# Hybrid Fourier / HGRN2 / mixture-of-experts layer: projections as single F32 products, and expert weights moved in transfers of one, two or four units

## The chip, the cores and the metric

The kernel runs on one core of one Trainium2 chip. The metric is the device time of one execution, in microseconds (us). TensorE is called PE below, its weight loads PEld, VectorE DVE, ScalarE ACT, GpSimd POOL, and the queue of SyncE, which issues nearly every load, SP.

## The reference

One layer over 512 latent rows and 256 context rows of width 1024, one sample, all in float32:

```
h_ctx = modulate(rms_norm(ctx, g_mix), sh1c, sc1c)
h_lat = modulate(rms_norm(x, g_mix), sh1, sc1)
u, q, v, gf, gb, g = split_proj(h @ w_in, lb)            # 1024 x 3072, for both streams
rec = rec_mixer(...)                                     # 4 heads, gated linear recurrence, two directions
mix = concatenate([fourier_mix(u, w_fourier), rec]) @ w_out
x = x + gt1 * mix
x = x + gt2 * ec_moe(modulate(rms_norm(x, g_ffn), sh2, sc2), w_router, w_g, w_u, w_d)
return rms_norm(x, g_final)

def ec_moe(h, w_r, w_g, w_u, w_d):                       # 16 experts, 64 tokens each
    affinity = softmax(h @ w_r)
    gate, idx = top_k(swapaxes(affinity, 1, 2), cap)
    xs = h[idx]
    hid = silu(xs @ w_g) * (xs @ w_u)                    # 1024 x 2816, twice
    ye = (hid @ w_d) * gate                              # 2816 x 1024
    return segment_sum(ye, idx)
```

The weights of the experts are 16 x 3 x 1024 x 2816 floats, 553.6 MB, and each is read once.

## The kernel before

The work falls into two parts. The **front** runs from the first load to the routing (0 to 372 us): the modulation of the rows by a product of the condition with `w_ada`, the input projection, the recurrence heads, the Fourier groups, the output projection, the router. The **experts** follow (372 us to the end).

*Projections.* The input projection goes by segments of 512 columns: q, vc (context rows of v), ff and fb (both streams), v, g, u, in this order, each in four steps of 256 channels. A step is cut into units: one 128x128 block of weights (or of rows) against 512 columns. Counted in such units there are q 32, vc 16, ff 32, fb 32, v 32, g 32, u 32 and, for the output projection, 64: 272 in all; ff and fb also have 32 products of 256 columns each with the context rows. Each operand is held as a high part, rounded to the type that PE takes in a single pass (F32R), and a low part, the rest; `mm3` (L144 to L147) makes each unit of three products, high by high, low by high and high by low. The parts of the weights are made by `split` and `split_tile`: a copy on ACT for the high part and a subtraction on POOL or DVE for the low one (L304 to L309). Raw weight tiles have four buffers, and so have the high and the low ones; a segment asks for the next step's tile when it begins a step.

*Order.* Three stretches are in an order that is written out by hand (`manual_schedule`): the opening (modulation, q, vc), the heads, and the PE stream of output projection, routing and first gate product. Between them the Tile framework orders the instructions. In the heads the units of v, g, u, the Fourier groups and part of the output projection are fillers: between two steps of the heads `fill_to(TURN)` takes units until PE has 3.0 us of work by the units' stated costs (0.65 us for a unit of a projection).

*Experts.* For each expert, eight units of gate weights, eight of up weights and eight of down weights come in; a unit is 128 partitions x 2816 floats (1.44 MB). They go through a ring of 13 equal slots, 7 in memory that the front's left side gives back and 6 on the right. SP issues a load when the slot's last reader is done. The order on PE within an expert is gate (L1403), up (L1403), transposes of the hidden rows (hT, L1435), down (dn, L1455), combination (cb, L1464); for every second expert the rows of two experts are gathered (gp, L1375). In memory a unit of gate or up is one contiguous block, 128 rows of 11264 bytes; a unit of down takes 11264 bytes out of each 45056. The last expert's down weights come by blocks of columns, in runs of 1024 and 512 bytes (`down_last`, L1488).

The context states (`ctx_states`) use two rotating buffers with the tag `gcc`, which the second part of the modulation uses before: POOL's memset of such a buffer waits for the transfer `gt2b` that still reads it.

Of the kernel before, what the change touches and what calls it, by code (L numbers as in the profile page):

```python
# [30 lines left out]
NSLOT_L = 7  # L31
NSLOT_R = 6
# [17 lines left out]
VC_AT = ((2, 6), (2, 7))  # L50

# columns of the packed small operands
# [8 lines left out]
# and of its matrices  # L61
# [4 lines left out]
# columns of the packed shape constants  # L66
# [16 lines left out]
def hybrid_kernel(ctx: ExitStack, tc, x, ctxt, small, const, pos, w_ada, b_ada, w_in, w_out,  # L83
                  wg, wu, wd, out):
# [12 lines left out]
    # ------------------------------------------------------------------ memory that stays  # L97
# [39 lines left out]
    def split_tile(w, name, low=None):  # L137
        wh = wst.tile([P, 2, 512], F32R, tag="wh", bufs=SB, name=f"{name}h")
        wl = wst.tile([P, 2, 512], F32R, tag="wl", bufs=SB, name=f"{name}l")
        ns.copy(wh, w)  # L140
        (low or nv).tensor_tensor(wl, w, wh.bitcast(F32), op=ALU.subtract)
        return wh, wl
# [6 lines left out]
    def pick(pair, sl):  # L149
        return (pair[0][sl], pair[1][sl])  # L150
# [25 lines left out]
    class AdaFirst:  # L176
        """Shift and scale of the mixer for channel blocks 2n and 2n+1."""

        def __init__(self, n):
            self.n = n  # L180
            if n % 2 == 0:
                # the memory of the values and of the context's gates
                w = p1b.tile([P, 2, 4, 256], F32, tag="v", name=f"adaw{n}_v")
                self.w = [w[:, 0], w[:, 1]] + [pc.tile([P, 4, 256], F32, tag=f"fctx{d}", name=f"adaw{n}_{d}")
                                               for d in range(2)]
            else:
                self.w = [wst.tile([P, 4, 256], F32, tag="wh" if t % 2 else "wl", bufs=SB, name=f"adaw{n}_{t}")
                          for t in range(4)]
            for t in range(4):
                # half of the rows of both halves of the sum  # L190
# [18 lines left out]
        def finish(self):  # L209
# [8 lines left out]
            # row r of the pair, shift or scale, channel block  # L218
# [10 lines left out]
    # ------------------------------------------------------------------ normalise and transpose  # L229
    # the transposed rows wait in the memory of the gates  # L230
# [28 lines left out]
    # high and low parts, channel blocks 4-7 and 0-3  # L259
    hlA = hl.tile([P, 2, 4, S], F32R, name="hlA")  # L260
    hl2 = tc.alloc_tile_pool(name="hl2", bufs=1, side="right")
    hlB = hl2.tile([P, 2, 4, S], F32R, name="hlB")

    def lat(k, sl=ALL):
        t = hlB if k < 4 else hlA
        return (t[:, 0, k % 4, sl], t[:, 1, k % 4, sl])

    hctx = (pc.tile([P, NK, CT], F32R, name="hctx_h"), pc.tile([P, NK, CT], F32R, name="hctx_l"))

    CTX_LOW = lambda k: ng if k % 2 else nv  # L270
    mods = pc.tile([P, 4, S], F32, tag="adaacc", name="mods")

    def modulate(k, r, between=None):
        src = xT[:, k, :S] if r == 0 else xT[:, k, S:]
        hi, lo = lat(k) if r == 0 else pick(hctx, (ALL, k))
        ns.activation(hi, src, AF.Identity, bias=sh1[:, r, k:k + 1], scale=a1[:, r, k:k + 1])
        m = mods[:, k % 4, :S if r == 0 else CT]
        nv.tensor_scalar(m, src, a1[:, r, k:k + 1], sh1[:, r, k:k + 1], op0=ALU.mult, op1=ALU.add)
        if between:
            between()  # L280
        (nv if r == 0 else CTX_LOW(k)).tensor_tensor(lo, m, hi.bitcast(F32), op=ALU.subtract)

    # ------------------------------------------------------------------ input projection
    class Segment:
        """Columns col..col+512 of the projection, four steps of 256 channels each."""

        def __init__(self, name, col, rows, with_ctx, low=None, with_lat=True):
            self.name, self.col, self.rows, self.with_ctx = name, col, rows, with_ctx
            self.with_lat = with_lat
            self.al, self.low = None, low  # L290
            self.loaded = {}
            self.parts = {}
            self.ahead, self.follow = False, None
            self.by_bank = BY_BANK

        def split(self, kk, a, high=None, low=None):
            """High and low parts of half a tile."""
            if kk not in self.loaded:
                self.load(kk)
            if a == 0:  # L300
                self.parts[kk] = [wst.tile([P, 2, 512], F32R, tag=t, bufs=SB, name=f"{self.name}{kk}{t}")
                                  for t in ("wh", "wl")]
            w, (wh, wl) = self.loaded[kk], self.parts[kk]
            (high or ns.copy)(wh[:, a], w[:, a])  # L304
            if low:
                low.tensor_tensor(wl[:, a], w[:, a], wh[:, a].bitcast(F32), op=ALU.subtract)
                return
            low = self.low[a] if isinstance(self.low, tuple) else ng
            low.tensor_tensor(wl[:, a], w[:, a], wh[:, a].bitcast(F32), op=ALU.subtract)  # L309

        def load(self, kk):
            self.loaded[kk] = load_seg(self.col, kk, f"{self.name}{kk}r")

        def units(self, kk):
            """One step, in units of one 128x128 block of weights against all its tokens."""
# [3 lines left out]
            if kk in self.parts:  # L319
                w2 = self.parts.pop(kk)  # L320
            else:
                if kk not in self.loaded:
                    self.load(kk)
                w2 = split_tile(self.loaded.pop(kk), f"{self.name}{kk}", self.low)
            def ahead(a):
                if self.ahead and kk + 1 < 4:
                    self.split(kk + 1, a)
                elif self.ahead and self.follow:
                    self.follow.split(0, a)

            def lat_unit(a, i):
                k, w = 2 * kk + a, pick(w2, (ALL, a))
                cb = slice(i * P, (i + 1) * P)
                l, r = (lat(k, cb), w) if self.rows else (pick(w, (ALL, cb)), lat(k))
                mm3(self.al[i], l, r, k == 0, k == NK - 1)

            def ctx_unit(a, b):
                k, w = 2 * kk + a, pick(w2, (ALL, a))
                st, sp = k == 0, k == NK - 1
                if self.rows:  # L340
                    mm3(self.ac[b], pick(hctx, (ALL, k, slice(b * P, (b + 1) * P))), w, st, sp)
# [1281 lines left out]
```

## Time and profile before

| | |
|---|---|
| median of 3 runs | 1671.04 us |
| lowest, highest | 1670.63, 1673.92 us |
| span of the profiled execution (first to last instruction) | 1668.7 us |
| PE busy, weight loads busy | 1529.1 us (92%), 753.1 us (45%) |
| DVE, ACT, POOL busy | 399.8 us, 255.9 us, 164.8 us |
| DMA | 608.37 MB, 365 GB/s over the span |
| chain that ended last | DMA 48%, PE 41%, DVE 5% |

The page has no time of its own for the profiled execution; its span lies 2.3 us below the median of the runs. A matmul's duration in the profile runs to a modelled end, so the pace of a stream of matmuls is read from their starts. A product of two F32 operands stands in the trace as two matmul instructions, one of two F32R operands as one.

### The profile page before, as it was taken

The numbers are of one execution on the slowest core, as the hardware profiler recorded it, in microseconds if no ns is written. First come the engines' busy times: TensorE is split into PE (matmuls) and PEld (weight loads), VectorE is DVE, ScalarE is ACT, GpSimd is POOL, SyncE is SP. The second block draws the span as 40 slices with busy tenths as digits, with TensorE's granted clock in tenths as the row PEclk, the third lists the DMA queues.
The fourth block names the chain that finished last, engine by engine and source line by source line (L and its number), as shares of the span: only waits on it lengthen the run. The fifth ranks groups of instructions, "written<-read, shape, count | busy, mean of one in ns | idle before, by whom it ended". The sixth has DMA issues, their size and how long they took to land.

```text
span 1668.7 us, 19918 instructions
## 1 busy us (share of the span) xinstructions
PE 1529.1 (92%) x8519; PEld 753.1 (45%) x8519; DVE 399.8 (24%) x754; ACT 255.9 (15%) x578; POOL 164.8 (10%) x153
## 2 busy tenths in 40 slices
PE   9978998989999999999898989988988899889897
PEld 6766776874443334343433343334333433243335
DVE  4855678370201010201011001100110111011103
ACT  4512456331000001000100010001000100010002
POOL 2623547400000000000000000000000000000002
PEclk9999999999999989999999998999999989999899
DMA  9785211859999999999999999999999999999998
GB/s 346 283 218 136 77 59 58 334 215 357 422 425 423 424 423 423 423 424 423 424 423 424 424 424 424 423 424 424 423 424 423 423 424 423 424 424 423 424 384 257
DMA packets 91448, 608.37 MB, mean 365 GB/s; under 512 B 8152, under 2 KB 30424, under 8 KB 41184
## 3 DMA queue, kind: packets, MB, share of 16 engines
q1 hardware_dynamic: 90480, 605.21, 88.6%
q10 hardware_dynamic: 880, 1.89, 1.5%
q8 instruction: 67, 1.10, 0.3%
q14 instruction: 21, 0.17, 0.0%
HBM read 604.18 MB, written 2.10 MB: 363 GB/s over the span
## 4 chain that ended last, share of the span: by engine, by line
DMA 48%; PE 41%; DVE 5%; ACT 2%; issue 1%; POOL 1%; SPq 0%; POOLq 0%; DVEq 0%; ACTq 0%
DMA uw<-in_wu_dram 18%; DMA gw<-in_wg_dram 15%; DMA dw<-in_wd_dram 12%; PE dn L1455 9%; PE g L1403 7%; PE u L1403 6%; PE gp L1375 4%; PE cb L1464 3%; DMA fb1r<-in_w_in_dram 1%; DMA adabuf<-in_w_ada_dram 1%; ACT xst L1377 1%; DVE X L795 1%; PE op L146 1%; PE op L145 1%; PE op L147 1%
## 5 line engine op out<-in xcount | busy, mean ns | idle before, releaser
L1455 PE MATMUL dn<-dw,hid 128*64 128x512 f32 (+1 forms) x1440 | 315.9, 562 | 9.0 <-DMA dw<-in_wd_dram 9.0
L1403 PE MATMUL u<-uw,xst 128*64 128x512 f32 (+1 forms) x1464 | 298.1, 559 | 23.4 <-DMA uw<-in_wu_dram 23.3
L1403 PE MATMUL g<-gw,xst 128*64 128x512 f32 (+1 forms) x1440 | 300.3, 569 | 0.0
L1403 PEld LDWEIGHTS u<-uw,xst 128*64 128x64 f32 x1464 | 102.7, 137 | 216.0 <-issue 165.1
L1455 PEld LDWEIGHTS dn<-dw,hid 128*64 128x64 f32 x1440 | 113.9, 136 | 168.1 <-issue 126.5
L1403 PEld LDWEIGHTS g<-gw,xst 128*64 128x64 f32 x1440 | 102.7, 139 | 187.0 <-issue 181.6
L1429 DVE TENSOR_TENSOR hid<-u,hid 128x512 f32<-128x512 f32 (+1 forms) x48 | 30.3, 647 | 538.5 <-PE u L1403 522.6
L1464 PE MATMUL cb<-ye,oht 64*128 64x512 f32 x240 | 108.9, 742 | 26.6 <-DVE acc_x L1467 15.6
L1415 ACT ACTIVATE hid<-g 128x512 f32<-128x512 f32 (+1 forms) x48 | 26.7, 561 | 655.2 <-PE g L1403 654.5
L1473 POOL COPY gt2f<-gt2b 64x512 f32<-64x512 f32 x2 | 1.2, 606 | 1265.8 <-DVE hid L1429 1265.8
L1375 PE MATMUL gp<-oh,xn 128*128 128x128 f32 x512 | 84.0, 294 | 23.3 <-ACT xst L1377 23.1
L1375 PEld LDWEIGHTS gp<-oh,xn 128*128 128x128 f32 x512 | 65.0, 190 | 74.5 <-issue 40.0
L1467 DVE TENSOR_TENSOR acc_x<-cb,acc_x 128x512 f32<-128x512 f32 x120 | 78.6, 688 | 57.6 <-PE cb L1464 57.6
L1377 ACT ACTIVATE xst<-gp,sh,a 128x128 f32<-128x128 f32 x64 | 29.3, 457 | 335.2 <-PE gp L1375 178.9
L1464 PEld LDWEIGHTS cb<-ye,oht 64*128 64x128 f32 x240 | 35.3, 206 | 97.2 <-DVE acc_x L1467 73.0
L1459 DVE TENSOR_TENSOR ye<-dn,gt2b 128x512 f32<-128x512 f32 x15 | 10.4, 692 | 214.9 <-PE dn L1455 214.9
L1437 ACT COPY hid<-hT 128x512 f32<-128x512 f32 (+1 forms) x48 | 24.8, 549 | 170.2 <-PE hT L1435 170.2
L1385 DVE TENSOR_TENSOR oh<-iota,posm 128x512 f32<-128x512 f32 x8 | 5.5, 692 | 182.8 <-PE gp L1375 182.7
L385 DVE SCALAR_TENSOR_TENSOR adaacc<-adabuf,cs,adaacc 128x1024 f32<-128x1024 f32 x28 | 44.3, 1642 | 5.1 <-DMA adabuf<-in_w_ada_dram 5.1
L1419 DVE TENSOR_SCALAR ohg<-iota,posm,aff 128x128 f32<-128x128 f32 x64 | 17.9, 343 | 103.2 <-PE ohT L1424 103.2
L1435 PE MATMUL hT<-ident,hid 128*128 128x128 f32 x176 | 29.3, 300 | 7.7 <-DVE hid L1429 5.9
L1435 PEld LDWEIGHTS hT<-ident,hid 128*128 128x128 f32 x176 | 23.9, 212 | 16.0 <-DVE hid L1429 11.6
(602 smaller groups left out, 1530.6 us busy)
## 6 DMA issues: line engine op xcount, KB each, us to landing
uw<-in_wu_dram SPq DMA_DIRECT2D x122, 1408.0 KB, 27.1
dw<-in_wd_dram SPq DMA_DIRECT2D x120, 1408.0 KB, 27.1
gw<-in_wg_dram SPq DMA_DIRECT2D x120, 1408.0 KB, 27.1
adabuf<-in_w_ada_dram SPq DMA_DIRECT2D x16, 1024.0 KB, 6.4
gw0a<-in_wg_dram SPq DMA_DIRECT2D x7, 1408.0 KB, 15.3
uw0a<-in_wu_dram SPq DMA_DIRECT2D x6, 1408.0 KB, 12.3
adaw<-in_w_ada_dram SPq DMA_DIRECT2D x24, 256.0 KB, 7.6
dw<-in_wd_dram SPq DMA_DIRECT2D x6, 768.0 KB, 13.9
```

Source lines behind the costliest of these rows:

```text
L385: nv.scalar_tensor_tensor(self.acc[:, a], w[:, a], cs[:, k, :1], self.acc[:, a], op0=ALU.mult, op1=ALU.add)
L1375: nt.matmul(gather.gp[:, o:o + P], lhsT=xn[:, i, k * P:(k + 1) * P], rhs=oh[:, i].rearrange("p a j -> p (a j)"), start=(i == 0), stop=(i = ...
L1377: ns.activation(xst[:, k].rearrange("p a j -> p (a j)"), gather.gp[:, o:o + P], AF.Identity, bias=sh2[:, k:k + 1], scale=a2[:, k:k + 1])
L1403: nt.matmul(b[i][64 * hf:64 * hf + 64, :n], lhsT=xst[:, k, e % 2, :], rhs=t[:, hf * HALF + c0:hf * HALF + c0 + n], start=(k == 0), stop=(k ...
L1415: ns.activation(hid[:, c0:c0 + n], gb[i][:, :n], AF.Silu)
L1419: nv.tensor_scalar(ohg[:, i], iota[:, None, :].to_broadcast([P, 2, CAP]), posm[:, i, e:e + 1], aff[:, i, e:e + 1], op0=ALU.is_equal, op1=A ...
L1429: nv.tensor_tensor(hid[:, c0:c0 + n], ub[i][:, :n], hid[:, c0:c0 + n], op=ALU.mult)
L1435: nt.transpose(tp[:, (r - r0) * P:(r - r0 + 1) * P], hid.rearrange("p (f r) -> p r f", r=NROW)[:, r, :], ident)
L1437: ns.copy(hidT[:, r0:r0 + n].rearrange("p r j -> p (r j)"), tp[:, :n * P])
L1455: nt.matmul(db[64 * dh:64 * dh + 64, c0:c0 + n], lhsT=hidT[:, r, 64 * ih:64 * ih + 64], rhs=t[:, o:o + n], start=(ih == 0 and r == 0), sto ...
L1464: nt.matmul(cb, lhsT=oht[hs, i * P:(i + 1) * P], rhs=ye[hs, :], start=True, stop=True, tile_position=(64 * dh, 0))
L1467: nv.tensor_tensor(acc_x[:, i, ds_], cb, acc_x[:, i, ds_], op=ALU.add)
```

## The change

1. `mm3` becomes `mm`: each unit is one product of F32 operands. The high and low parts, their tiles, the copies and the subtractions are gone; modulation writes one tile, alternately by ACT and DVE. The rows of the heads (`mr`) and of the Fourier groups (`mf`) go into the output projection as they are.
2. Raw weight tiles have 8 buffers, and a step asks for the tile three steps ahead, across segments.
3. The stated cost of a filling unit is 0.43 us; the residual gate's columns (`gate_cols`) are all scaled on POOL.
4. Gate and up weights lie in memory by partition: the eight units of a partition stand one behind another. Experts 0 and 1 are loaded by single units, 2 and 3 by pairs, 4 to 14 by fours, the last one's gate by fours, its up by pairs. Down weights keep their place. The ring is three blocks of four units and a spare one, which single units alone use.
5. The last expert's down weights are an input of their own, laid out in the order of their blocks.

```diff
-NSLOT_L = 7
-NSLOT_R = 6
+NSLOT_L = 8
+NSLOT_R = 5
+SINGLE, PAIR, QUAD = (1, 1, 1), (2, 2, 2), (4, 4, 4)
+BURST = [SINGLE] * 2 + [PAIR] * 2 + [QUAD] * 11 + [(4, 2, 1)]
+AHEAD = 3
...
-    RB, SB = 4, 4
+    RB, SB = 8, 4
...
-    def mm3(o, a, b, start, stop):
-        nt.matmul(o, lhsT=a[0], rhs=b[0], start=start, stop=False)
-        nt.matmul(o, lhsT=a[1], rhs=b[0], start=False, stop=False)
-        nt.matmul(o, lhsT=a[0], rhs=b[1], start=False, stop=stop)
+    def mm(o, a, b, start, stop):
+        nt.matmul(o, lhsT=a, rhs=b, start=start, stop=stop)
...
+        def load_ahead(self, kk):
+            seg = self
+            while seg and kk > 3:
+                seg, kk = seg.follow, kk - 4
+            if seg:
+                seg.load(kk)
...
-                w2 = split_tile(self.loaded.pop(kk), f"{self.name}{kk}", self.low)
+            self.load(kk)
+            w2 = self.loaded.pop(kk)
+            self.load_ahead(kk + AHEAD)
...
-                    c = next(self.q[0][1]) or 0.65
+                    c = next(self.q[0][1]) or 0.43
...
-            if n in (0, 2):
-                gate_cols(k, n // 2, nv if k < 3 else ng)
-            elif n in (3, 5):
-                split_high(k, n // 4)
-            elif n in (4, 6):
-                split_low(k, n // 6, ng)
+            if n in (0, 4):
+                gate_cols(k, n // 4, ng)
...
+    quads = [wl_pool.tile([P, 4 * DE], F32, name=f"wl{i}") for i in range(NSLOT_L // 4)]
+    quads.append(wr_pool.tile([P, 4 * DE], F32, name="wr0"))
+    spare = wr_pool.tile([P, DE], F32, name="wr1")
...
+    def load_unit(w, e, u):
+        key = (w, e, u)
+        if key not in ahead:
+            n = BURST[e]["gud".index(w)]
+            t = area(n)
+            if w == "d":
+                nc.sync.dma_start(t, wds[e, u // 4, :, u % 4 * DE:(u % 4 + n) * DE])
+            else:
+                nc.sync.dma_start(t, {"g": wg, "u": wu}[w][e, :, u * DE:(u + n) * DE])
+            for i in range(n):
+                ahead[w, e, u + i] = t[:, i * DE:(i + 1) * DE]
+        return ahead.pop(key)
...
+    by_partition = lambda w: w.reshape(NE, NK, P, DE).transpose(0, 2, 1, 3).reshape(NE, P, NK * DE)
```

## Rows read from the trace of the kernel before

**Rows 1.** Busy time by stretch (us, then instructions), granted clock, DMA share, GB/s.

```profile
18.00:110.00 92.00, 89.13 (x520) 68.73 (x519) 61.78 (x83) 35.97 (x63) 41.64 (x30) 1.00 0.87 277
110.00:150.00 40.00, 31.41 (x189) 28.09 (x188) 24.05 (x26) 10.10 (x18) 14.32 (x10) 0.91 0.75 233
150.00:176.00 26.00, 18.47 (x89) 14.26 (x89) 9.53 (x12) 6.64 (x13) 6.43 (x7) 0.87 0.41 33
176.00:302.00 126.00, 113.31 (x1456) 88.87 (x1455) 92.27 (x159) 74.69 (x212) 70.60 (x63) 0.99 0.21 64
302.00:356.00 54.00, 53.52 (x284) 44.75 (x282) 27.67 (x89) 18.64 (x42) 15.47 (x16) 1.00 0.74 307
...
400.00:1600.00 1200.00, 1113.62 (x5233) 440.09 (x5233) 147.88 (x262) 73.94 (x146) 0.00 (x0) 0.98 1.01 423
```

**Rows 2.** Timeline of PE in the output projection, first and last of 24 products.

```profile
316.95 0.39 PE L145 MATMUL op<-wo0wh,hlA 128*128 128x512 f32 x1
...
322.17 0.39 PE L147 MATMUL op<-wo3wl,hlA 128*128 128x512 f32 x1
```

**Rows 3.** Two F32 products of 512 columns: durations, first and last start.

```profile
L969 PE MATMUL abp<-smm,cst x4: 591/592/593, 275.6 to 276.9; 128*128 128x512 f32 x4
```

**Rows 4.** Timeline of PE: twelve products of 256 columns; four F32 products of 257.

```profile
129.80 0.28 PE L145 MATMUL fb_c<-hctx_h,fb1wh 128*128 128x256 f32 x1
...
131.05 0.28 PE L147 MATMUL fb_c<-hctx_l,fb1wh 128*128 128x256 f32 x1
...
284.61 2.01 PE L1000 MATMUL fp<-ptab,fdt 128*128 128x257 f32 x8
286.46 1.03 PE L1016 MATMUL fo<-pq,ab 128*128 128x257 f32 x4
```

**Rows 5.** What PE waited for from 100 to 300 us: total, times, longest.

```profile
PE fb_c L145 <- ACT fctx L526: 8.6, 1, 8.6
PE v_l L147 <- POOL v1wl L309: 7.5, 1, 7.5
```

**Rows 6.** The chain that ended last: start us, us, what.

```profile
69.28 4.60 DVE adaacc L385 x3
...
94.39 23.32 DMA fb1r<-in_w_in_dram
...
118.93 0.51 ACT fctx L526
...
153.30 10.69 DMA gt2b<-adag
```

**Rows 7.** DMA from 700 to 1500 us: packets in all, then SP's queue (packets, MB, share).

```profile
DMA packets 33827, 338.85 MB, mean 424 GB/s; under 512 B 3756, under 2 KB 3756, under 8 KB 3756
...
q1 hardware_dynamic: 33794, 338.36, 100.7%
```

**Rows 8.** DMA from 303 to 316 us, the same rows.

```profile
DMA packets 791, 5.44 MB, mean 418 GB/s; under 512 B 48, under 2 KB 48, under 8 KB 457
```

**Rows 9.** DMA from 1628 to 1648 us, the same rows.

```profile
DMA packets 7647, 6.54 MB, mean 327 GB/s; under 512 B 165, under 2 KB 7645, under 8 KB 7645
```

**Rows 10.** Timeline of PE in an expert of the middle.

```profile
839.86 1.13 PE L1464 MATMUL cb<-ye,oht 64*128 64x512 f32 x4 [0.79 <-DVE ye L1459]
...
847.23 7.31 PE L1403 MATMUL g<-gw,xst 128*64 128x512 f32 x36
...
867.21 19.06 PE L1403 MATMUL u<-uw,xst 128*64 128x512 f32 x96
887.01 1.25 PE L1435 MATMUL hT<-ident,hid 128*128 128x128 f32 x8 [0.73 <-DVE hid L1429]
```

**Rows 11.** Groups by line and shape: busy us, mean ns, idle before and its releaser.

```profile
L1375 PE MATMUL gp<-oh,xn 128*128 128x128 f32 x512 | 84.0, 294 | 23.3 <-ACT xst L1377 23.1 <-DVE oh L1385 0.2
...
L1500 PE MATMUL dq<-dw,hid 128*64 128x256 f32 x132 | 16.8, 384 | 0.5 <-DMA dw<-in_wd_dram 0.5
```

**Rows 12.** SP's queue before the experts.

```profile
322.62 33.85 SPq L1354 DMA_DIRECT2D uw0a<-in_wu_dram  x6
```

More of the change, by code (lines that the diff above doesn't have):

```diff
@@ L270, in hybrid_kernel @@
-    CTX_LOW = lambda k: ng if k % 2 else nv
-    mods = pc.tile([P, 4, S], F32, tag="adaacc", name="mods")
-    def modulate(k, r, between=None):
-        src = xT[:, k, :S] if r == 0 else xT[:, k, S:]
[L275 to L281, printed above, removed]
+        return (hlB if k < 4 else hlA)[:, k % 4, sl]
@@ L288, in __init__, with load @@
             self.name, self.col, self.rows, self.with_ctx = name, col, rows, with_ctx
             self.with_lat = with_lat
-            self.al, self.low = None, low
+            self.al = None
             self.loaded = {}
-            self.parts = {}
-            self.ahead, self.follow = False, None
+            self.follow = None
             self.by_bank = BY_BANK
-        def split(self, kk, a, high=None, low=None):
+        def load(self, kk):
             if kk not in self.loaded:
[L299 to L309, printed above, removed]
@@ L356, in units @@
                     order += [(lat_unit, a, i) for i in range(nl)] + [(ctx_unit, a, b) for b in range(nx)]
-            for n, (unit, a, i) in enumerate(order):
-                if n in (0, len(order) // 2):
-                    ahead(int(n > 0))
+            for unit, a, i in order:
                 unit(a, i)
@@ L662, in until @@
                 self.take(1)
-    sv.ahead = sg.ahead = su.ahead = True
-    sv.follow, sg.follow = sg, su
     gg = p1b.tile([P, NH, S], F32, tag="gg", name="gg")
@@ L698, in hybrid_kernel @@
     ph = tc.alloc_tile_pool(name="ph", bufs=1, side="left", reuse_waits="tile")
-    mr = pk.tile([P, 2, NH, S], F32R, tag="rows", name="mr")
-    mrh = [mr[:, 0, h, :] for h in range(NH)]
-    mrl = [mr[:, 1, h, :] for h in range(NH)]
+    mr = pk.tile([P, NH, S], F32, tag="rows", name="mr")
     HEADS = {}
@@ L900, in head_out @@
         yield
[L901 to L907 removed]
+    raws = {}
     def load_out(k):
@@ new lines, in hybrid_kernel, with area @@
+    quads.append(wr_pool.tile([P, 4 * DE], F32, name="wr0"))
+    spare = wr_pool.tile([P, DE], F32, name="wr1")
+    unit_of = [quads[u // 4][:, u % 4 * DE:(u % 4 + 1) * DE] for u in range(12)] + [spare]
+    at = [0]
+    ahead = {}
+    def area(n):
+        if n == 1 and not area.bursts:
+            u = at[0] % 13
+            at[0] += 1
+            return unit_of[u]
+        if not area.bursts:
+            assert at[0] % 13 == 8
+            area.bursts, at[0] = True, 8
+        u = at[0] % 12
+        assert u % n == 0
+        at[0] += n
+        return quads[u // 4][:, u % 4 * DE:(u % 4 + n) * DE]
@@ L1357, in hybrid_kernel, with load_ahead @@
+    def load_ahead(w, u, t=None):
+        if t is None:
+            t = area(1)
+        nc.sync.dma_start(t, {"g": wg, "u": wu}[w][0, :, u * DE:(u + 1) * DE])
+        ahead[w, 0, u] = t
     for k in range(NK - 1):
-        load_ahead(wg, "g", k)
-    for k in range(nslot - NK + 1):
-        load_ahead(wu, "u", k)
+        load_ahead("g", k)
+    for k in range(13 - NK + 1):
+        load_ahead("u", k)
     pe = tc.alloc_tile_pool(name="pe", bufs=1, side="right", reuse_waits="tile")
-    load_ahead(wg, "g", NK - 1, pe.tile([P, DE], F32, tag="hid", name="first"))
+    load_ahead("g", NK - 1, pe.tile([P, DE], F32, tag="hid", name="first"))
@@ L1391, in hybrid_kernel, with up @@
                     gather(xst, oh, e, k)
-        def up(w, name, first=False):
-            b = [bank("acc", f"{name}{e}_{i}") for i in range(3)]
+        def up(w, first=False):
+            b = [bank("acc", f"{w}{e}_{i}") for i in range(3)]
             if first:
```

175 lines of the change are left out of this document (51 added, 124 removed).

## Prediction

> **What bounds the kernel now.** I read the busy times by stretch first [rows 1]. They split the run in two. From 400 to 1600 us the 16 DMA engines are full (share 1.01, 423 GB/s) while PE is busy for 1114 of 1200 us. That the experts are bound by DMA is seen again in the packets: from 700 to 1500 us SP's queue moved 33794 - 3756 = 30038 packets of 11264 bytes, so one takes 800 us x 16 / 30038 = 426 ns of an engine [rows 7]. In the front the shares are the other way round: PE is busy for 89.1 of 92 us (18 to 110 us), 113.3 of 126 (heads) and 53.5 of 54 (output projection), with DMA at 0.87, 0.21 and 0.74. The front delays the experts one for one: only a ring of 13 units and one more can be loaded ahead, and the last six of them are issued from 322.6 us on, over 33.9 us [rows 12], before the first gate product. So the sum is: growth of the front, plus change of the stream's length, plus the tail.
>
> **Change 1, the products.** In the output projection 24 F32R products start between 316.95 and 322.17 us: 23 steps of 0.227 us, so a unit of three takes 0.681 us [rows 2]. An F32 product of 512 columns is in the trace, two of them as four instructions that start from 275.6 to 276.9 us: 3 steps of 0.43 us, 0.87 us a product [rows 3]. The other bound is the experts' up product, 8 units in 867.21 to 887.01 less the 0.73 us idle, 2.38 us for 1408 columns in pairs, which is 0.87 us for 512 as well [rows 10]; with the idle and the last drain it is 0.90. I take 0.87: +0.19 us a unit (to +0.22). For 256 columns, twelve products in 129.80 to 131.05 make 11 steps of 0.114, 0.341 us for three; four F32 products of 257 columns take 1.85 us, 0.46 each [rows 4]: +0.12.
>
> So one product costs more than three, and PE gets longer by stretch:
>
> - 18 to 110 us (q 32, vc 16, ff 32, fb 8 units, 32 narrow products): 88 x 0.19 + 32 x 0.12 = +20.5
> - 110 to 150 (fb 24, 32 narrow): +8.4
> - 150 to 176 (v 16): +3.0
> - heads (v 16, g 32, u 32): +15.2
> - output projection (64): +12.2
>
> Together +59 us. What it takes away: the copies and subtractions of the parts. They lie on ACT, POOL and DVE, none of which is full in any stretch (DVE 92 of 126 us in the heads [rows 1]), so they count only where PE waited for them.
>
> **What comes back.** From 94 to 119 us the chain goes through the load of `fb1r`, 23.3 us, its high part on ACT, then the context gates behind it on ACT [rows 6]; PE waited 8.6 us for these gates [rows 5]. ACT executes in order, and with no copy of weights in its queue the gates no longer stand behind the load; besides, the load is asked for three steps ahead into 8 buffers. The wait goes whole, and with it some 1.2 us in which the twelve products behind it ran at half pace (granted clock 0.91 in this stretch against 1.00 in the next to it [rows 1]): -9.8. Next, 7.5 us for `v1wl` on POOL [rows 5]: that subtraction stood behind a memset which waits for `gt2b`, 10.7 us [rows 6]. The subtraction goes, but the memset and the scan of the context's gates behind it stay, and after 12 units PE needs them; I take -5 (0 to -7.5). The opening has 2.9 us of idle PE, partly for parts of weights and of rows: -2.3. In the heads PE was idle for 12.7 us, most of it waits of the scores for ACT and DVE. Filling units are now priced at 0.43 and take 0.87, so early steps get about 2.45/0.43 = 5.7 units instead of 3.8 and PE has work for 5 us where the heads' chain needs some 3: it no longer waits there, but the fillers run out sooner, and the last head's steps stand bare. From this I take -7, and -3 for the Fourier groups, which move forward from the tail of the heads into their middle. The output projection has 0.5 us of idle PE [rows 1], and the routing none that the change touches. Sum -27; **front +32 us**, between +10 and +45: the lower end, if the heads hide all their growth beside the returns already counted; the upper, at 0.22 a unit and half of the returns.
>
> POOL has to scale all columns of the gate, but loses two subtractions for each of them, so it has less to do. SP gets past the weights' loads earlier: with 8 buffers they wait for no subtraction.
>
> **Change 2, the stream of weights.** No weight packet in these rows is longer than 11264 bytes; the cost of a longer one is bounded from two pairs of rows, as a fixed part and one by length. From 1628 to 1648 us the queue is full of 1024-byte packets: 7480 in 20 us, 42.8 ns each [rows 9]. With 426 ns for 11264 bytes that makes 4.5 ns + 37.4 ns per 1000 bytes; a run of 45056 bytes takes 1691 ns where four take 1704: -0.8%. From 303 to 316 us some 409 packets of 4096 and 333 of 11264 pass; less 333 x 426 ns, one of 4096 takes 162 ns [rows 8]: 11 ns + 36.9, and the long run 1671 ns: -2.0%. By fours come 392 MB (925 us at 424 GB/s), by pairs 81 MB (190 us; -0.5 or -1.3%). The gain is 8 or 21 us. It is nothing if the queue cuts runs anyway. The second pair is nearer in size, but its stretch is short: I take **-14** (0 to -21).
>
> Can PE follow? A block of four units takes it 4 x 2.5 = 10 us [rows 10], its transfer 13.4. Pauses are the combination, 7.4 us (839.86 to 847.23 [rows 10]), and for every second expert the gather, 84 + 23 us over 8 pairs, 13 us [rows 11]. With three blocks, transfer n may start when block n-3 is read. If a block lands at 0, PE is done with it at 10, combines until 17.5 and has read the first gate block at 27.5; that block's memory is wanted at 40. If the gather falls just before it as well, it is 40.5, some 2 us late with the issue, once in two experts. So the ring holds, barely in that case, which costs 2 us x 6.
>
> **The tail.** The last up weights come by pairs, so two units instead of one are left after the last landing: +2.5 [rows 10]. The shorter load of the last down weights gains nothing: its products waited 0.5 us for DMA [rows 11].
>
> **Sum.** 1668.7 (the profiled span) + 32 - 14 + 2.5 = 1689; the median of the runs lies 2.3 us above that span: **1691 us**.
>
> The Trainium skill ("DMA: Bandwidth & Descriptors", "Measured") has 425 GB/s for a transfer of 16 MB, 97% of what it gives as the fabric's ceiling, and asks for 1 MiB per transfer. The 424 GB/s of [rows 7] with transfers of 1.44 MB agree. By that, longer transfers would bring nothing; the packets of [rows 8] speak for a little more.
>
> **Rivals.**
>
> *The stream gains nothing* (the queue cuts the runs, or the rest lost is not per packet): 1691 + 14 = 1705. For it: between 4096 and 11264 bytes the pace changes by few per cent only, and 0.8% is the other reading.
>
> *The growth of PE is hidden, the kernel is faster.* The chain goes through DVE's sums for the modulation before 94 us [rows 6], and the heads' steps are DVE's too (92 of 126 us busy [rows 1]). If these, not PE, set the pace from 63 to 150 us and in the heads, only the first 48 units (+9) and the output projection (+12) grow; with -27 and -14 + 2.5 it is 1671 - 17.5 = 1653. It decides when PE's true idle time in these stretches exceeds its growth; 2.9 of 92 and 12.7 of 126 us [rows 1] speak against it, though a matmul's modelled end hides some idle time.
>
> *The coarser ring stalls.* If PE's order puts gather and combination together in front of the gate, or a wait stands for a whole block, the stream stops for 3 to 8 us in each of six pairs or more: 1710 to 1740. PE's 86 us of slack in 1200 [rows 1] speak against it.
>
> *Front and stream cancel*: front +12, stream -14: about 1671.
>
> **How the numbers follow.** The forecast (1680 to 1702) 0.45, no gain in the stream 0.20, growth hidden 0.14, ring stalls 0.13, cancelled 0.08. The range takes in the forecast, the case without gain, half of the stalls, the cancelled case and part of the hidden one: 1664 to 1714. A change under 0.2% (3.3 us) can't be told from none here: faster 0.17 (hidden, and a little of cancelled), same 0.07, slower 0.76.
>
> **What the changed profile would show.** F32 units of the projections at two instructions of 0.43 us; the first gate product some 30 us later than 372; no wait of PE for `fctx` at 8 us; DMA from 700 to 1500 us at 427 to 432 GB/s, with a quarter of the packets or less; PE waiting 2 to 3 us at a time for a block of four. I am wrong if an F32 unit starts every 0.6 us, if the heads take no longer than now, or if the DMA share in the experts falls below 0.98.

## The result, and the profile after

The changed kernel takes 1700.1 us (median of 4 runs, 1695.8 to 1704.1) against 1672.1 for the one before: ratio 1.0164, interval 1.0144 to 1.0185. It is slower by 1.6%. Its profiled span is 1697.2 us, 28.5 more than before. Three starts of PE split this sum:

| | before | after | measured | predicted |
|---|---|---|---|---|
| first gate product (front) | 373.7 | 408.7 | +35.0 | +32 |
| first gate to last up product (stream) | 1250.0 | 1244.5 | -5.5 | -14 |
| last up product to the end (tail) | 45.0 | 44.0 | -1.0 | +2.5 |

So all of what was lost lies in the front, and the stream gave back less than half of what it should.

Busy time by stretch after the change, to be read against [rows 1]:

```profile
18.00:110.00 92.00, 92.00 (x367) 46.65 (x367) 34.40 (x55) 17.57 (x28) 2.21 (x4) 1.00 0.87 305
110.00:150.00 40.00, 35.31 (x117) 21.92 (x116) 20.86 (x26) 3.36 (x6) 0.63 (x2) 0.96 0.79 182
150.00:176.00 26.00, 26.00 (x94) 14.30 (x93) 6.36 (x13) 6.63 (x11) 0.10 (x1) 1.00 0.35 47
...
193.60:340.70 147.10, 138.14 (x1403) 80.09 (x1403) 70.10 (x158) 58.44 (x178) 31.08 (x38) 0.98 0.16 55
340.70:388.60 47.90, 47.90 (x185) 26.55 (x183) 18.14 (x72) 11.72 (x29) 9.81 (x10) 1.00 0.59 241
```

PE is now the only full engine of the front: 92.00 of 92 us busy in the opening, while POOL falls from 41.64 to 2.21 and DVE from 61.78 to 34.40. The work that was taken away had not been PE's.

The pace of the F32 products, in PE's timeline after (eight instructions are four products):

```profile
122.79 3.62 PE L142 MATMUL fb_c<-hctx,fb0r 128*128 128x256 f32 x16
126.24 3.60 PE L142 MATMUL fb_l<-hlB,fb1r 128*128 128x512 f32 x8
129.68 1.03 PE L142 MATMUL fb_c<-hctx,fb1r 128*128 128x256 f32 x4
135.39 1.11 PE L517 MATMUL kcT<-ident,gcc 128*128 128x128 f32 x4 [4.69 <-DVE gcc L510]
```

From 126.24 to 129.68 us are 0.86 us a product of 512 columns, from 122.79 to 126.24 us 0.43 us one of 256. The last row is a wait that was not there before. What PE waited for from 20 to 400 us, to be read against [rows 5]:

```profile
PE kcT L517 <- DVE gcc L510: 7.7, 2, 4.7
PE fp L933 <- ACT fdt L924: 3.3, 1, 3.3
```

The waits for `fctx` and `v1wl` are gone. In their place the transposes of the context's gates wait for DVE, 4.7 us at 135 us and 3.0 us at 183 us.

The stream from 700 to 1500 us, in forty slices of 20 us, to be read against [rows 7]:

```profile
GB/s 433 431 431 433 431 431 433 431 433 401 427 431 433 429 431 433 433 413 365 433 433 433 432 431 433 433 427 431 433 431 431 433 431 433 305 433 431 433 431 433
DMA packets 8520, 340.49 MB, mean 426 GB/s; under 512 B 944, under 2 KB 944, under 8 KB 944
...
q1 hardware_dynamic: 8491, 340.04, 98.8%
```

SP's queue needs a quarter of the packets. By share of time and bytes the engines spend 0.988 x 16 x 800 us / 340.04 MB = 37.2 us on a MB, before 1.007 x 16 x 800 / 338.36 = 38.1: 2.4% less; by the rate of the full slices, 432 GB/s against 424, it is 1.8%. In most slices the rate is 431 to 433 GB/s, but some fall to 401, 365 and 305: there the queue ran dry. Counted by the packets of the trace, the stretches from the first gate product to the last up product in which at most 8 of the 16 engines were busy sum to 13.4 us. Before, counted alike, they are some 5 us, 3.4 of them right behind the first gate product. Of the 13.4 us, 3.6 lie at 411, 439 and 573 us, ahead of the blocks of four. The longest, 5.2 us, in PE's timeline:

```profile
1339.13 9.71 PE L1391 MATMUL dn<-wl,hid 128*64 128x512 f32 x48
1348.77 0.71 PE L1312 MATMUL gp<-oh,xn 128*128 128x128 f32 x4
...
1357.44 9.71 PE L1391 MATMUL dn<-wl,hid 128*64 128x512 f32 x48
1367.94 1.13 PE L1400 MATMUL cb<-ye,oht 64*128 64x512 f32 x4 [0.79 <-DVE ye L1395]
1369.85 8.16 PE L1400 MATMUL cb<-ye,oht 64*128 64x512 f32 x12 [0.78 <-DVE acc_x L1403]
1377.93 11.14 PE L1340 MATMUL g<-wr,xst 128*64 128x512 f32 x48
1389.01 0.66 PE L1361 MATMUL ohT<-ident,ohg 128*128 128x128 f32 x4
```

The issues of SP's queue in the same stretch:

```profile
1348.87 0.33 SPq L1283 DMA_DIRECT2D wl<-in_wg_dram  x1
1367.19 0.33 SPq L1283 DMA_DIRECT2D wl<-in_wu_dram  x1
1389.12 0.33 SPq L1283 DMA_DIRECT2D wr<-in_wu_dram  x1
```

Each block is freed, and loaded anew, when PE has read its fourth unit: at 1348.8 (first half of down), 1367.1 (second half) and 1389.0 us (first half of gate). Between the second and the third lie the combination and a gate block, 22 us, and between the first and the second the rest of the gather. That is 40 us for two loads of some 13 us each and what was still under way at 1348.9 us: the queue was empty from 1385.1 to 1390.3 us.

Five times PE goes this way from the first to the third release with all blocks of four, each time with the same 153 matmul instructions. The five stretches (busy time, granted clock, DMA as in [rows 1]):

```profile
859.03:898.05 39.02, 34.53 (x153) 14.93 (x154) 8.44 (x15) 2.29 (x5) 0.00 (x0) 0.91 0.97 420
1022.74:1061.76 39.02, 34.53 (x153) 14.79 (x154) 8.44 (x15) 2.29 (x5) 0.00 (x0) 0.91 0.96 413
1186.29:1222.43 36.14, 31.47 (x153) 14.14 (x154) 8.25 (x15) 2.29 (x5) 0.00 (x0) 1.00 1.02 438
1348.87:1389.12 40.25, 35.95 (x153) 15.27 (x154) 8.54 (x15) 2.29 (x5) 0.00 (x0) 0.87 0.89 383
1514.14:1550.28 36.14, 31.47 (x153) 14.14 (x154) 7.56 (x14) 2.29 (x5) 0.00 (x0) 1.00 1.00 429
```

Where the granted clock is 1.00, the way takes 36.1 us and the queue is empty for 0.4 us at most. Where a part of it runs at 1.2 instead of 2.4 GHz (means of 0.91 and 0.87), it takes 39.0 to 40.3 us, and the queue is empty for 1.1, 3.1 and 5.2 us. So with blocks of four the queue runs dry where the gather and the lower clock come together; in e5_price, e6_near and e11_rows_after, too, every gap of more than 1.5 us lies within 10 us of such a fall's end. In all five PE does the same ahead of the gap: the rest of the gather, the second half of down, and the start of the combination with two waits of 0.8 us. Why the clock fell in three of them is not shown.

### The profile page after: what moved, and what is told of

Its sections match the earlier page's. It is cut to its first block, busy times and chain, and to the rows that moved or that the text cites. A ratio compares the mean times of both kernels' runs of the same rounds, so it can differ in the third digit from the quotient of the medians.

```text
span 1697.2 us, 18508 instructions
## 1 busy us (share of the span) xinstructions
PE 1558.7 (92%) x8183; PEld 715.6 (42%) x8183; DVE 337.6 (20%) x713; ACT 210.5 (12%) x492; POOL 62.3 (4%) x86
## 4 chain that ended last, share of the span: by engine, by line
PE 70%; DMA 20%; DVE 4%; issue 3%; ACT 3%; POOL 0%; POOLq 0%; ACTq 0%; DVEq 0%
PE g L1340 15%; PE dn L1391 14%; PE u L1340 11%; DMA wl<-in_wd_dram 9%; DMA wr<-in_wu_dram 9%; PE cb L1400 6%; PE gp L1312 4%; PE op L142 3%; PE q_l L142 2%; PE u_l L142 2%; PE g_l L142 2%; DVE acc_x L1403 2%; ACT xst L1314 1%; DMA adabuf<-in_w_ada_dram 1%; PE dq L1437 1%
## 5 line engine op out<-in xcount | busy, mean ns | idle before, releaser
L1391 PE MATMUL dn<-wl,hid 128*64 128x512 f32 (+1 forms) x1416 | 294.6, 565 | 17.8 <-DMA wl<-in_wd_dram 17.8
L1391 PEld LDWEIGHTS dn<-wl,hid 128*64 128x64 f32 x1416 | 116.3, 138 | 174.4 <-issue 134.7
L1340 PE MATMUL u<-wr,xst 128*64 128x512 f32 (+1 forms) x792 | 167.8, 579 | 16.4 <-DMA wr<-in_wu_dram 16.4
L1340 PE MATMUL g<-wl,xst 128*64 128x512 f32 (+1 forms) x816 | 166.1, 559 | 0.0
L1340 PE MATMUL u<-wl,xst 128*64 128x512 f32 (+1 forms) x744 | 150.6, 557 | 3.7 <-DMA wl<-in_wu_dram 3.6
L1340 PE MATMUL g<-wr,xst 128*64 128x512 f32 x708 | 150.9, 580 | 0.0
L1340 PEld LDWEIGHTS u<-wr,xst 128*64 128x64 f32 x792 | 61.0, 142 | 120.7 <-issue 96.5
L1340 PEld LDWEIGHTS g<-wl,xst 128*64 128x64 f32 x816 | 58.5, 137 | 96.8 <-issue 94.1
L1340 PEld LDWEIGHTS u<-wl,xst 128*64 128x64 f32 x744 | 54.5, 137 | 96.1 <-issue 84.9
L1340 PEld LDWEIGHTS g<-wr,xst 128*64 128x64 f32 x708 | 51.6, 143 | 102.2 <-issue 101.3
L1314 ACT ACTIVATE xst<-gp,sh,a 128x128 f32<-128x128 f32 x64 | 29.3, 457 | 319.7 <-PE gp L1312 162.8
```

Source lines behind the costliest of these rows:

```text
L1314: ns.activation(xst[:, k].rearrange("p a j -> p (a j)"), gather.gp[:, o:o + P], AF.Identity, bias=sh2[:, k:k + 1], scale=a2[:, k:k + 1])
L1340: nt.matmul(b[i][64 * hf:64 * hf + 64, :n], lhsT=xst[:, k, e % 2, :], rhs=t[:, hf * HALF + c0:hf * HALF + c0 + n], start=(k == 0), stop=(k ...
L1391: nt.matmul(db[64 * dh:64 * dh + 64, c0:c0 + n], lhsT=hidT[:, r, 64 * ih:64 * ih + 64], rhs=t[:, o:o + n], start=(ih == 0 and r == 0), sto ...
```

## The experiments

All times are medians of four runs, ratios against the kernel before on the same chip; `after` means the changed kernel.

| kernel | us | ratio, 95% interval | first gate | stream | starved |
|---|---|---|---|---|---|
| after | 1700.1 | 1.0164, 1.0144 to 1.0185 | 408.7 | 1244.5 | 13.4 |
| e1_front | 1705.7 | 1.0199, 1.0183 to 1.0214 | 409.4 | 1249.9 | |
| e3_singles | 1705.2 | 1.0196, 1.0181 to 1.0212 | 408.7 | 1250.6 | 0.7 |
| e4_pairs | 1693.4 | 1.0126, 1.0109 to 1.0143 | 408.8 | 1240.6 | 3.8 |
| e5_price | 1692.0 | 1.0119, 1.0104 to 1.0134 | 401.4 | 1246.6 | 14.8 |
| e2_stream | 1662.0 | 0.9945, 0.9930 to 0.9959 | 375.1 | 1240.7 | |
| e6_near | 1712.5 | 1.0244, 1.0223 to 1.0265 | 412.0 | 1253.6 | 10.3 |
| e7_nogather | 1687.7 | 1.0096, 1.0075 to 1.0118 | 408.1 | 1235.9 | 0.9 |
| e8_onepass | 1645.5 | 0.9853, 0.9830 to 0.9877 | 343.3 | 1253.1 | |
| e9_rows | 1651.8 | 0.9884, 0.9868 to 0.9901 | 365.2 | 1241.5 | |
| e10_both | 1691.4 | 1.0121, 1.0106 to 1.0136 | 400.6 | 1244.8 | 6.9 |
| e11_rows_after | 1695.7 | 1.0136, 1.0109 to 1.0164 | 402.5 | 1252.3 | 18.2 |
| e12_all | 1685.2 | 1.0072, 1.0055 to 1.0089 | 400.1 | 1239.8 | 3.4 |

First gate, stream and starved (at most 8 of 16 engines busy, from the first gate product to the last up product) are from the profiled execution, in us.

**The two halves, each alone.** e1_front has the new projections with the experts of before; e2_stream the front of before with the new layout, in blocks of two:

```diff
+BURST = [SINGLE] * 2 + [PAIR] * 13 + [(2, 2, 1)]
...
+    pairs = [(wl_pool if i < 3 else wr_pool).tile([P, 2 * DE], F32, name=f"w{i}") for i in range(6)]
+    spare = wl_pool.tile([P, DE], F32, name="w6")
```

> The projections as single F32 products, with the experts of the kernel before: slots, layout and single transfers unchanged. My theory: the front alone makes the kernel slower, so that the first gate product comes 33 to 36 us later than in the kernel before and the time is 33 to 37 us above it (1705 us, ratio 1.021); the stream from the first gate product to the last up product stays at 1250 us. Rival: the growth of the front comes from the new ring, whose first loads wait for a larger piece of memory; then this kernel is within 10 us of the one before.

> The front of the kernel before (three products a unit, parts of weights), with the new layout and pairs of units in six blocks and a spare one for experts 2 to 15. My theory: front and stream add up, so the first gate product stays at 373 to 375 us and the stream takes 1240 to 1242 us as in the changed kernel with pairs: 1662 us, 9 to 10 us faster than the kernel before (ratio 0.994). Rival: with a front that is 35 us shorter the first loads are not yet there, or the stream's gain needs the changed front; then the time is within 3 us of the kernel before.

Both came as expected. Change 1 alone costs 33.6 us, and the layout alone, in blocks of two where the change has four, gives 9.2 us: one change is a loss and the other a gain. In e1 the stream is that of before to 0.1 us, so the later front is passed on whole.

**Size of the blocks.** The changed kernel with single units throughout:

```diff
-BURST = [SINGLE] * 2 + [PAIR] * 2 + [QUAD] * 11 + [(4, 2, 1)]
+BURST = [SINGLE] * 16
```

and with pairs from the third expert on:

```diff
+BURST = [SINGLE] * 2 + [PAIR] * 13 + [(2, 2, 1)]
```

> The changed kernel with every transfer a single unit, so that the layout by partition stays and the long runs go. My theory: what the stream gains is a fixed cost per packet, so without long runs it is back at the pace of 426 to 429 ns for 11264 bytes and has no stalls of a coarse ring: 1250 us from the first gate product to the last up product, time 5 to 8 us above the changed kernel (1706 us). Rival: the layout itself sets the pace, by the distance of a partition's rows: then the packets of gate and up differ from those of down, and the time lies more than 10 us from the changed kernel, either way.

> The changed kernel with pairs of units for experts 2 to 15 in place of fours. A run of 22528 bytes took 846 ns on average against half of 1676, so the pace of the packets loses about 10 us over eleven experts; my theory says that the ring in six blocks loses nearly none of the 12 us for which the stream stood still, so the time is within 4 us of the changed kernel, with under 3 us of starved stream. Rival: the still stretches come from PE being too slow, not from the blocks' size; then they stay and the kernel is 8 to 12 us slower than the changed one.

The layout in memory does nothing by itself (1250.6 against 1250.0 us). Pairs are 6.7 us better than fours by the medians, where at most 4 were expected, and 3.8 us in the profiled executions. The starved time is 3.8 us and not under 3, but it lies at 411, 439 and 573 us, where both kernels still move single units and pairs; behind that the blocks of two are never dry. The shorter runs cost 5.7 us (1686 ns for two packets against 1676 for one, 8704 times, 16 engines) and save 9.6 us of empty queue, which is about the 3.9 us by which the stream is shorter. The stream of e4_pairs from 700 to 1500 us:

```profile
GB/s 426 427 431 431 431 428 427 425 429 430 433 430 429 427 425 429 431 431 430 428 424 430 430 429 430 433 425 426 430 430 428 431 431 423 429 431 429 428 431 430
...
q1 hardware_dynamic: 17106, 342.66, 100.2%
```

The undisturbed rate is lower than with fours (1.002 x 16 x 800 / 342.66 = 37.4 us for a MB against 37.2), but no slice is below 423 GB/s, and the mean is higher.

**What empties the queue.** The changed kernel, leaving out the gathers of pairs 1 to 7:

```diff
-            xst = pe.tile([P, NK, 2, CAP], F32, tag="xst", name=f"xst{e}")
-            if e > 0:
-                for k in range(NK):
-                    gather(xst, oh, e, k)
+            if e == 0:
+                xst = pe.tile([P, NK, 2, CAP], F32, tag="xst", name=f"xst{e}")
```

> The changed kernel without the gathers of expert pairs 1 to 7 (they use the rows of the first pair): 13 us of PE's work a pair left out. My theory: the stream of fours stands still because gather and combination lie between the last down block and the next gate block, so without the gather the starved time falls from 13 us to under 4 and the stream from the first gate product to the last up product is 9 to 12 us shorter (time 1689 us). Rival: the blocks of four cost the stream by themselves (issue and landing of a block); then the starved time stays over 8 us and the time within 4 us of the changed kernel.

The starved time falls from 13.4 to 0.9 us and the time by 12.4 us. The mean granted clock of this run is lower than that of the changed kernel (0.949 against 0.970), and still the queue does not run dry behind 440 us for more than 0.3 us at a time: the blocks of four alone do not empty it, nor does the lower clock alone. The gather has to be there, and in the changed kernel the three larger gaps have the lower clock as well. The stream is then 14.1 us shorter than before; that this is the prediction's -14 is chance, since that sum had other terms (below).

**The price of a filling unit.**

```diff
-                    c = next(self.q[0][1]) or 0.43
+                    c = next(self.q[0][1]) or 0.87
...
-                yield 0.43
+                yield 0.87
```

> The changed kernel with a filling unit priced at what it takes, 0.87 us instead of 0.43. My theory: PE's total work sets the length of the heads, not its distribution; fewer fillers per step let the heads' chain run ahead, and the fillers are left for the tail, so the front changes by less than 5 us either way. Rival: the wrong price makes a good part of the front's growth, since the last head's steps stand bare; then the front is 10 us or more shorter than in the changed kernel.

The first gate product comes 7.3 us sooner, between the two. PE's rows of e5_price for its heads and its output projection:

```profile
194.80:311.30 116.50, 112.18 (x1331) 65.64 (x1331) 68.01 (x141) 54.82 (x168) 28.65 (x31) 1.00 0.15 51
311.30:382.40 71.10, 71.10 (x256) 39.56 (x255) 23.23 (x90) 15.65 (x40) 14.19 (x17) 1.00 0.47 192
```

In the heads PE idles 4.3 us here, 9.0 in the changed kernel (the row from 193.60 above) and 12.7 before (123.3 us from 179.0 to 302.3, of which 110.6 busy). At half its true price a unit is handed out too freely, and too few are left for the last steps: PE's waits for `fdt` and `y` in the heads, 3.3 and 2.4 us in the changed kernel, are 0.3 us each here. What the true price leaves over runs without a gap behind the heads. Of the 7.4 us that heads and output projection get shorter, 4.7 are idle time; for the rest PE is busy for 2.8 us less, at a granted clock of 1.00 in the heads where the changed kernel has 0.98.

**Buffers and early loads.** Four raw buffers and one step ahead, as before the change:

```diff
-AHEAD = 3
+AHEAD = 1
...
-    RB, SB = 8, 4
+    RB, SB = 4, 4
```

> The changed kernel with four raw weight buffers instead of eight and the next step's tile asked for instead of the third one on. My prediction put the end of the 8.6 us wait to the missing copies on ACT and, besides, to the early loads. If the copies alone held the gates, the time stays within 3 us of the changed kernel; if the early load is what counts, PE waits for a weight tile (fb1r above all, which took 23 us in the kernel before) and the front grows by 5 to 15 us.

Up to the end of the heads every start agrees with the changed kernel's to 0.1 us (116 us for `fb`, 166.3 for `v`, 340.7 for the last `o`), and the wait for `fctx` stays away. That does not tell the copies from the late load, though, since no load is late here: `fb1r` is asked for at 93.7 us, as before (94.4), but it is there by 97 us instead of 117.7 [rows 6]. DMA of e6_near from 93 to 98 us, in slices of 0.125 us:

```profile
GB/s 459 328 66 66 0 0 0 0 0 0 0 0 0 66 213 98 16 98 180 115 180 229 393 393 393 426 410 426 295 197 33 33 0 0 0 0 0 0 0 0
```

In the kernel before, the load ran beside `gt1b`, which ACT's queue issues at 95.9 us; that queue from 94 to 118 us (packets, MB, share of the 16 engines' time):

```profile
q10 hardware_dynamic: 288, 0.52, 60.9%
```

In e6_near `gt1b` is issued at 105.8 us, behind the load's landing, and PE comes to `fb1r` at 126 us. Whether the missing copies, the load's landing or the later PE ended the wait stays open. What is lost, 12.4 us, lies behind the heads: 3.3 us up to the first gate product, where the output projection waits for POOL's scaled columns (3.7 us in all), and 9.1 us in the stream, because SP's queue gets to the ring late. Neither of the two expected cases came. The issues of SP's queue in the changed kernel:

```profile
341.76 3.54 SPq L1291 DMA_DIRECT2D wl<-in_wg_dram  x7
...
389.22 2.33 SPq L1291 DMA_DIRECT2D wr<-in_wu_dram  x5
```

The same issues in e6_near, 10 and 20 us later:

```profile
351.79 4.70 SPq L1291 DMA_DIRECT2D wl<-in_wg_dram  x7
...
409.35 2.37 SPq L1291 DMA_DIRECT2D wr<-in_wu_dram  x5
```

**Is PE the bound of the front?** The kernel before with the high by high product alone, 138 us of PE's work less:

```diff
-        nt.matmul(o, lhsT=a[0], rhs=b[0], start=start, stop=False)
-        nt.matmul(o, lhsT=a[1], rhs=b[0], start=False, stop=False)
-        nt.matmul(o, lhsT=a[0], rhs=b[1], start=False, stop=stop)
+        nt.matmul(o, lhsT=a[0], rhs=b[0], start=start, stop=stop)
```

> The kernel before with only the product of the high parts, so two of three products of every unit are left out (544 of 512 columns at 0.227 us and 128 of 256 at 0.114: 138 us of PE's work), all parts still being made. If PE alone set the front, the first gate product would come 110 us earlier or more; if other chains (the sums for the modulation, the heads' steps on DVE) lie close behind PE, 30 to 70 us. I expect 50 us: time about 1620 us. Rival (growth hidden): under 15 us.

The front gets only 30.4 us shorter, at the lower edge of 30 to 70, and the time is 1645 us instead of 1620. What PE waits for from 18 to 400 us in this kernel:

```profile
PE sc L755 <- ACT km L714: 14.0, 11, 2.0
PE fb_l L145 <- ACT fb1wh L302: 12.2, 1, 12.2
PE ff_l L145 <- ACT ff3wh L302: 10.1, 1, 10.1
```

From 18 us to the first gate product of this kernel:

```profile
18.00:343.30 325.30, 221.35 (x1980) 162.25 (x1978) 238.50 (x433) 151.86 (x358) 150.06 (x126) 0.82 0.61 203
```

With 138 us of work left out PE is busy for 98 us less (319.7 us before, up to 373.7 us), since the granted clock is 0.82 where it was 0.97. So PE bounds the front upwards above all: of the 55 us that the change adds, 35 are paid, and of 138 us taken away a fifth comes back. ACT's copies and the heads' chain lie close behind it, and the clock was lower; how much each of them took is not separated.

**The shared rows.** e2_stream, and then the changed kernel, with the modulation's row in memory of its own:

```diff
-            row = pc.tile([P, 512], F32, tag="gcc", bufs=2, name=f"adag{g}")
+            row = pc.tile([P, 512], F32, tag="adrow", bufs=1, name=f"adag{g}")
```

> The kernel before's front with the new layout by pairs (0.9945 of before in its own run), and one more edit: the row of the second part of the modulation has memory of its own, so that the memset for the context's gates no longer waits for the transfer gt2b. Theory (the 7.5 us wait of PE for v1wl comes from that shared memory): v starts 5 to 7.5 us sooner, the first gate product 4 to 7.5 us sooner, time 1655 to 1658, ratio 0.990 to 0.992. Rival (the wait only moves on to the next load or scan): first gate product within 2 us of where it was, 1661 to 1663.

> The changed kernel with the one edit that gave the front of before 9.9 us: the row of the second part of the modulation in memory of its own. In the changed kernel the transposes of the context's gates wait twice, 4.7 us at 135 us, behind a sum on DVE that waits for a load of w_ada, and 3.0 us at 183 us, behind the transfer gt2b. Theory: only the second goes (the first has nothing to do with the shared memory), with a little of the slower clock behind it: first gate product 3 to 5 us sooner, 1695 to 1698. Rival (the change only shifted the same wait, both go): 7.5 to 10 us, 1690 to 1693.

In e9 the gain is 10.3 us, more than the wait of 7.5 us and more than expected. The stretch from 150 to 176 us in e2_stream:

```profile
150.00:176.00 26.00, 18.47 (x90) 14.33 (x90) 9.87 (x14) 6.19 (x11) 6.30 (x6) 0.80 0.39 31
```

The same stretch in e9_rows:

```profile
150.00:176.00 26.00, 25.85 (x227) 20.42 (x226) 13.60 (x19) 11.03 (x22) 12.10 (x11) 1.00 0.51 72
```

With the wait goes the granted clock of 0.80, that is, part of the stretch at 1.2 instead of 2.4 GHz. In the changed kernel the wait at 183 us disappears and the one at 135 us stays (4.5 us), as the theory had it; the first gate product comes 6.2 us sooner, a little more than the theory's 3 to 5. The time itself doesn't settle it: its interval overlaps that of the changed kernel, and its four runs lie between 1689.3 and 1700.8.

**All together.** Pairs and price, and then the row as well, in the changed kernel:

> The changed kernel with blocks of two units in place of four and the filling units priced at 0.87 us, what one takes. If the two edits act on stretches that have nothing to do with each other (heads and ring), their gains add: 6.7 + 8.1 us off the changed kernel's 1700, so 1685, ratio 1.0075 to 1.009. If the gain by the price came from more time for the first loads of the ring, it is lost partly with smaller blocks: 1688 to 1692.

> The changed kernel with all three edits: rows in memory of their own, filling units priced at what they take, blocks of two units. If the row's edit adds to the 1691.4 of the other two: 1687 to 1689, ratio 1.009 to 1.011. It then stays above before, and the whole excess is the front's. If the three together remove all waits that the change brought, 1680 or less.

e10 is no better than price alone (1691.4 against 1692.0): it has pairs, but 4.2 us more stream than e4. That is the length by which a gap at 565 us has grown: 5.7 us, 5.8 in e5_price, 1.6 in e4. The stretch from 550 to 568 us in e10_both:

```profile
550.00:568.00 18.00, 16.44 (x44) 5.15 (x42) 6.72 (x10) 0.00 (x0) 0.00 (x0) 0.72 0.84 358
```

The same stretch in e12_all:

```profile
550.00:568.00 18.00, 16.07 (x64) 5.46 (x62) 7.56 (x14) 0.00 (x0) 0.00 (x0) 1.00 0.94 388
```

The gap goes with the granted clock: 0.72 in e10_both and in e5_price, 1.00 in e4_pairs and in e12_all, whose gap is 1.2 us although its experts start no later (400.1 us, e10_both 400.6). So an earlier start does not make the gap, and the time of e10 within 1688 to 1692 is no evidence for the rival that was written down for it. Why the clock fell there is not shown. All three edits give 1685.2, a little below the 1687 to 1689 expected and still 0.7% above before: the front stays 26.4 us longer, the stream is 10.2 us shorter. The best version is e9_rows, the three products kept: 1651.8 us, 1.2% below before.

## Why the prediction was near, and where it was off

The direction, the bound and the account by front and stream held: 1700.1 lies in the forecast's own range of 1680 to 1702, 9 us above its number. That the sum came so near is in part luck: the front was 3 us and the tail 3.5 us off in opposite directions, and in the stream the gain by long runs was put too low and the ring's cost left out. By its steps:

- *The price of a unit* held: 0.87 us was taken, 0.86 measured; for 256 columns 0.46 and 0.43. By the measured prices (272 x 0.18 + 64 x 0.09) the growth is 55 us, not 59.
- *What comes back* was 20 us instead of 27, so the front grew by 35. Start by start (the predicted values are growth less returns): up to `fb` +12.0 (predicted 16.7), across `fb` +4.3 (0.1), from `v` to the heads' first product -1.7 (-2), heads and output projection +19.0 (17.4), routing to first gate +1.4 (0). At the measured prices the stretch of `fb` gave back 4.3 us and not 9.8, heads and output projection 6.9 and not 10. The `fctx` wait went (the text's reason for it is not shown, see e6_near), but 4.7 us of it came back as the first wait for `gcc`: those gates stand on DVE behind a sum that waits for a load of `w_ada`. The memset behind `gt2b` stayed, as said, and cost 3.0 us. In the heads the idle time fell by 3.7 us, not by 7; the fillers did run out, and the price of 0.43 was behind it (e5_price).
- *The rate of long runs* was right in kind and put too low: the text had -8 us from one pair of rows and -21 from the other, and took -14 between them. By the rates of the full slices (432 GB/s with fours and 429 with pairs against 424) the long runs give some -19 us, by the packets' own durations -24. The pair of rows nearest in size [rows 7, 8] had it about right, and the bound of -0.8% from 1024-byte packets [rows 9] is refuted, as is the rival that the queue cuts the runs. The Trainium skill ("DMA: Bandwidth & Descriptors", "Measured") gives 425 GB/s, 97% of the ceiling, for a transfer of 16 MB, which the prediction read as nothing left to gain; the measurement decides: 431 to 433 GB/s in most slices, closer to the 435 that the same page gives as the ceiling ("Where 436 GB/s comes from").
- *The ring* is the other mis-sized term: it stood at nothing in the sum, and the empty queue cost some 8 us more than before; the stream, -14 in the sum, measured -5.5. The text worked out that the gather beside the combination takes 40.5 us from one block's landing to the release of the third, "some 2 us late", 2 us x 6, and left those 12 us out of the sum. That the starved time is 13.4 us looks like these 12, but by chance. At the full clock the way takes 36.1 us (8.7 of the gather's 13 us lie in it), and then the ring holds; 39.0 to 40.3 us came where the granted clock fell, which the text did not reckon with. Three of five pairs lost 9.4 us so, and 3.6 us lie ahead of the blocks of four. The rival "the coarser ring stalls" thus came true in kind, at 1.1 to 5.2 us in three pairs, below its price of 3 to 8 us in six or more.
- *The tail* was costed at +2.5 and came out at -1.0; the two units after the last landing lie ahead of the last up product, so within the stream here (4.5 us from that landing to that product, 2.1 before). The -1.0 is found in every kernel with the new layout (44.0 to 44.2 us) and in none without it (44.8 to 45.3): it goes with the last down weights' layout, which was not tried alone.
- *Growth hidden behind DVE* is refuted by the front's +35 us and by the opening, where PE shows no idle time at all.

Of the signs named, an F32 unit at two instructions of 0.43 us, no wait for `fctx`, and a quarter of the packets came as said. PE's waits for blocks came as well, 14 of them from 420 to 1640 us, 2.5 us in the mean:

```profile
PE dn L1391 <- DMA wl<-in_wd_dram: 17.8, 7, 3.6
PE u L1340 <- DMA wr<-in_wu_dram: 13.7, 5, 3.7
PE u L1340 <- DMA wl<-in_wu_dram: 3.6, 2, 1.8
```

DMA's mean is 426, just below the 427 to 432 that was named.

The terms of the stream, added up: long runs -24 us by the packets' own durations (8704 of 45056 bytes in 1676 ns where four take 1715, and 3584 of 22528 bytes in 846 where two take 858); early single units at 438 ns instead of 429, +2.6; some 90 units more still to be moved at the first gate product, +2.5; empty queue, some +8. That makes -11 where -5.5 was measured. Most of the rest is that the recorded times of neighbouring packets overlap: added up over 16 engines, the stream's packets take 1254 us before and 1234 after, which with the empty time is some 9 us more than the stream's length before and 3 more after. A packet's duration thus overstates what the long runs save by about a quarter.

## What to carry to other kernels

Before three cheap passes are replaced by one dear one, look at which engine is full: it is of no use to unload ACT, POOL and DVE where PE is the bound, and a price given to a hand-written filler must be changed with the work that it stands for. A ring needs more than the mean balance: add up the longest run of PE's work between the releases of neighbouring blocks, pauses included and with the lower clock allowed for, and put what exceeds the transfers that are queued into the sum, not into a rival. Smaller blocks in the same memory can win although each transfer is a little slower. And a gain as large as that of the new layout (10.3 us against 9.2) may lie in a shared buffer that shows in the profile as a wait for something else.

## What the hardware showed that was not expected

- A run of 45056 bytes takes 1676 ns of a DMA engine, one of 22528 bytes 843 (e4_pairs), one of 11264 bytes 429. Per unit that is 419, 422 and 429 ns: two units have three quarters of what four gain.
- The times spread over 8.3 us with fours (1695.8 to 1704.1), 2.4 with pairs (1693.0 to 1695.4), 1.7 with single units (1704.1 to 1705.7). Of the four runs with fours the fastest has the highest mean granted clock (0.977), the two slowest the lowest (0.965 and 0.962). The ring alone is not the reason: e8_onepass, with the ring of before, spreads over 9.6 us, e7_nogather over 6.8.
- The same 153 matmul instructions take 36.1 us at the full granted clock and up to 40.3 us where it falls to 1.2 GHz for a part: behind the fall at 1370 us twelve products of the combination took 8.16 us and a gate block 11.14 instead of 9.67 (at 1212.7 us), in the very stretch on which the next release waited.
